# Scores of the dilated head pairs: second and third batch in one step, without projection products between them

## The chip, the cores and the metric

The kernel runs on one core of a Trainium2 chip (trn2). The metric is device time in microseconds (us): the median of three runs is 1185.5 us (1185.36 to 1185.55). One more execution was taken by the hardware profiler, and all rows below are from it. The engines are named as the profile names them: PE (TensorE, matrix products; PEld is its weight load), DVE (VectorE), ACT (ScalarE), POOL (GpSimd, nearly unused here) and SP (SyncE, which only issues transfers).

## What is computed

A decoder trunk of two layers for 512 tokens of width 1024, in float32. Layer 0 is attention and a convolutional feed-forward network, layer 1 a gated linear recurrence and another such network. The change lies in the attention of layer 0. Its queries, keys and values come from one projection of the normalised input; queries and keys are normalised per head. There are two kinds of heads:

```
oa = dilated_mixture_attention(qa, ka, va, slopes[:8])       # 8 heads of 64
ob = differential_attention(qb, kb, vb, slopes[8:], lam)     # 4 heads, two score maps each
y  = concatenate([oa, rms_norm(ob) * (1 - lam_init)]) @ w_out
```

Each dilated head mixes three windowed softmaxes. For 512 tokens the mixture is one causal softmax with an added bias for distance and for the number of windows that hold a position, and so the kernel computes it: scores q k^T, plus bias, row maximum, exponential, row sum, division, product with v.

## The kernel before

All large products are made in three parts: each operand is split into a rounded high part and a remainder (hi, lo), and PE adds hi·hi, hi·lo and lo·hi in a PSUM bank. Weights stream from HBM in units; ACT makes the high part (`wh`, line 106), DVE the remainder (`wl`, line 108).

**The attention stage as one line of steps.** The 8 dilated and 8 differential score maps are handled as 8 pairs. `ORDER = (4, 5, 6, 7, 0, 1, 2, 3)` puts four differential pairs first, then four dilated pairs, called D0, D1, D2 and D3 from here on. The backbone of PE's order is a list of *groups*: for each pair 16 groups of six projection products (`pj`, line 361), four groups to each of four weight units. The last four groups of a pair complete its four PSUM accumulators, one for each block of 128 tokens. While one pair is projected, the attention steps of the pair before are put between the groups, at places that a table gives, counted in groups from the pair's end:

```
BATCHES = ((0, 1), (2,), (3,))
PLACES = dict(qk=9, sc=(12, 14, 16), tr=(18.5, 20.7, 23.5, 25.2), step=1, out=27.3, norm=29)
```

D3 has a table of its own, `LAST`, with tighter places; beside it run the first products of the attention's output projection (`mm<-oh`, lines 127 to 129), three to a step. PE runs the list in just this order (`keep_in_program_order`). ACT and DVE get their order from a scheduler that follows the program, and that puts the evacuation of projections ahead (`high_priority`).

**One score batch** (`sc`, then `products`, lines 447 to 467). For a block of 128 query tokens there are three parts by two heads; the two heads lie on partitions 0 to 63 and 64 to 127 and write two banks. So a batch is six matmuls with a 64-row operand for each block. The first batch holds blocks 0 and 1 (128 and 256 keys), the second block 2 (384), the third block 3 (512). Each call of `products` takes two banks of the PSUM pool `pa`, which has four in all. The same pool serves the transposes of queries and keys (`qkt`), the transposes of the probabilities (`pt`), the products with v (`O`) and the row means of the differential pairs (`obms`). A tile keeps its bank until its last reader is done.

**Softmax of a row block** (`softmax_row`, line 475): DVE reads the score bank, adds the bias and keeps the negated row maximum (one instruction, followed by a short read of the accumulator, `mx`); ACT takes the exponential and the row sum; DVE the reciprocal; ACT scales. Once DVE has read a block's scores, the bank is free.

**What else ACT and DVE do there.** The evacuation of each finished projection accumulator is an ACT copy (`qkraw`, line 380), an ACT scaling (`v`, line 394) and a DVE remainder (`v`, line 395). After two accumulators, ACT squares them (`sq`, line 411) and DVE sums the squares (`ms`, line 412). Of the pair before, the second head's product with v (`O`) is read by ACT (`t`, line 561) and then by DVE (`o`, line 562).

Of the kernel before, what the change touches and what calls it, by code (L numbers as in the profile page):

```python
# [30 lines left out]


BATCHES = ((0, 1), (2,), (3,))
PLACES = dict(qk=9, sc=(12, 14, 16), tr=(18.5, 20.7, 23.5, 25.2), step=1, out=27.3, norm=29)
LAST = dict(qk=7.5, sc=(9.8, 10.5, 11.2), tr=(12.7, 13.4, 14.2, 15), step=0.35, out=16.2, norm=18)

# [28 lines left out]
def trunk(  # L65
# [30 lines left out]
    def nm(s):  # L96
        uid[0] += 1
        return f"{s}{uid[0]}"

    def bank(s):  # L100
        return pa.tile([P, S], F32, tag="pa", name=nm(s))
# [124 lines left out]
    with ExitStack() as actx:  # L226
# [73 lines left out]
        tiles = [{} for _ in ORDER]  # L300

        def pe(ins):

            return tc.keep_in_program_order(ins)
# [136 lines left out]
        def where(n):  # L441
            return LAST if n == NT - 1 else PLACES

        def head_bias(h):
            bt = ap2.tile([P, S], F32, tag="bias", name=nm("bias"))
            if h < 8:
                V.scalar_tensor_tensor(bt, dist_a, -SLOPES[h], lnc, ALU.mult, ALU.add)
            else:
                V.tensor_scalar(bt, dist_b, -SLOPES[h], None, ALU.mult)
            return bt  # L450

        def products(qk, blocks):


            (qh, ql), (kh, kl) = qk
            banks = (bank("S"), bank("S"))
            res, at = {}, 0
            for i in blocks:
                n = (i + 1) * P
                qs = slice(i * P, (i + 1) * P)  # L460
                for j, (q, k) in enumerate(((qh, kh), (ql, kh), (qh, kl))):
                    for s in range(2):
                        hs = slice(s * HD, (s + 1) * HD)
                        pe(T.matmul(banks[s][:, at : at + n], q[hs, qs], k[hs, :n], start=j == 0, stop=j == 2))  # L464
                for s in range(2):
                    res[s, i] = banks[s][:, at : at + n]
                at += n
            return res

        def softmax_row(ps, i, bt):  # L470

            n = (i + 1) * P
            e = smp.tile([P, n], F32, tag=f"sm{i}", name=nm("sm"))
            mx = tiny.tile([P, 1], F32, tag="mx", name=nm("mx"))
            V.tensor_tensor_reduce(out=e[:, :n], in0=ps, in1=bt[:, S - n :], scale=-1.0, scalar=3e38,
                                   op0=ALU.add, op1=ALU.min, accum_out=mx)
            sm = tiny.tile([P, 1], F32, tag="sum", name=nm("sum"))
            A.activation(e[:, :n], e[:, :n], AF.Exp, scale=-1.0, bias=mx, accum_out=sm)  # L478
            V.reciprocal(sm, sm)
            return e, sm  # L480

        def transposed(e, i, pth, ptl):
            ps = bank("pt")
            for b in range(i + 1):
                pe(T.transpose(ps[:, b * P : (b + 1) * P], e[:, b * P : (b + 1) * P], ident))  # L485
            src = ps[:, : (i + 1) * P].rearrange("p (b q) -> p b q", q=P)
            sl = slice(i, i + 3 * i + 1, 3)
            A.copy(pth[:, sl], src)
            return V.tensor_tensor(ptl[:, sl], src, pth[:, sl].bitcast(F32), ALU.subtract)

        def pv(out, v, pth, ptl, s=None):

            def product(b, v_cols, p, rows, start, stop):
                q = slice(b * P, S)
                rhs = p[:, 4 * b : 3 * b + NB].rearrange("p b q -> p (b q)")
                pe(T.matmul(out[rows, q], v[:, b, v_cols], rhs, start=start, stop=stop))  # L496


            every, hi, lo = slice(0, P), slice(0, P), slice(P, 2 * P)
            if s is None:  # L500
                for b in range(NB):
                    product(b, hi, pth, every, b == 0, False)
                    product(b, lo, pth, every, False, False)
                for b in range(NB):
                    product(b, hi, ptl, every, False, b == NB - 1)
            else:
                both, high = slice(s * P, (s + 1) * P), slice(s * P, s * P + HD)
                for b in range(NB - 1):
                    product(b, both, pth, every, b == 0, False)
                for b in range(NB):  # L510
                    product(b, high, ptl, slice(0, HD), False, False)
                product(NB - 1, both, pth, every, False, True)

        def pt_tiles():
            return (ap2.tile([P, 13, P], F32R, tag="pth", name=nm("pth")),
                    ap2.tile([P, 13, P], F32R, tag="ptl", name=nm("ptl")))

        def o_tiles(p):
            hi = actp.tile([P, S], F32R, tag=f"ah{p}", name=nm("oh"))
            lo = actp.tile([P, S], F32R, tag=f"al{p}", name=nm("ol"))  # L520
            oT[p] = (hi, lo)
            return hi, lo

        def attn_a(n):

            p = ORDER[n]
            st = {}

            def sc(blocks):
                if blocks[0] == 0:  # L530

                    with ExitStack() as order:
                        if n - 1 in rows_done:
                            order.enter_context(tc.issue_after(rows_done[n - 1].ins))
                        st["b"] = [head_bias(2 * p + s) for s in range(2)]
                rows = products(tiles[n]["qk"], blocks)
                for i in blocks:
                    for s in range(2):
                        e, r = softmax_row(rows[s, i], i, st["b"][s])
                        if n == NT - 1 and i == NB - 1:  # L540

                            V.tensor_scalar(e, e, r, None, ALU.mult)
                        else:
                            A.activation(e, e, AF.Copy, scale=r)  # L544
                        st["e", s, i] = e

            def tr(s, i):
                if i == 0:
                    st["pt", s] = pt_tiles()
                last = transposed(st["e", s, i], i, *st["pt", s])  # L550
                if i == 1:
                    rows_done[n] = last

            def out(s):
                ps = bank("O")
                pv(ps, tiles[n]["v"], *st["pt", s], s)
                if s == 0:
                    st["o"] = smp.tile([P, S], F32, tag="o", name=nm("o"), bufs=1)
                    st["t"] = smp.tile([P, S], F32, tag="t", name=nm("t"), bufs=1)
                lo_half, own = ((ps[HD:], slice(0, HD)), (ps[:HD], slice(HD, P)))[s]  # L560
                A.copy(st["t"][own], lo_half)
                V.tensor_tensor(st["o"][own], ps[own], st["t"][own], ALU.add)
                if s == 1:
                    hi, lo = o_tiles(p)
                    A.copy(hi, st["o"])
                    V.tensor_tensor(lo, st["o"], hi.bitcast(F32), ALU.subtract)

            at = where(n)
            steps = [(g, partial(sc, b)) for g, b in zip(at["sc"], BATCHES)]
            steps += [(g + s * at["step"], partial(tr, s, i)) for i, g in enumerate(at["tr"]) for s in range(2)]  # L570
            return steps + [(at["out"] + s * at["step"], partial(out, s)) for s in range(2)]

        def attn_b(n):
# [52 lines left out]
            at = where(n)  # L626
            steps = [(g, partial(sc, b)) for g, b in zip(at["sc"], BATCHES)]
            steps += [(g, partial(tr, i)) for i, g in enumerate(at["tr"])]
# [26 lines left out]
        at = {}  # L655
# [17 lines left out]
        for n in range(NT):  # L673
            end = 16 * n + 15
# [354 lines left out]
```

## Time and profile before

| | |
|---|---|
| Median of three runs | 1185.5 us |
| The profiled execution | 1184.98 us |
| Its span (first to last instruction) | 1183.2 us |
| PE busy | 1177.0 us, 99% of the span |
| DVE, ACT busy | 812.6 us (69%), 584.7 us (49%) |
| Attention stage | about the first 230 us |
| Granted TensorE clock, mean | 0.999 of full speed |

The timeline view gives, for each instruction, its start from the span's beginning, its duration, engine, line, operation, what it writes and reads, its shape, and in brackets the idle time of the engine before it and what ended that. Durations of matmuls overlap (the engine is pipelined), so the pace of PE is read from the differences of starts. An instruction that appears with `x2` stands for two equal ones in a row: the two heads.

### The profile page before, as it was taken

To read this page: it belongs to the slowest core of one execution; us is meant where nothing else is said; L and a number is where in the kernel's file an instruction comes from. 1 tells how busy PE (TensorE), PEld (TensorE's weight loads), DVE (VectorE), ACT (ScalarE), POOL (GpSimd) and SP (SyncE) were. 2 spreads that over 40 slices of the span, in tenths; PEclk is the share of its full clock that TensorE was granted. 3 is DMA by queue.
4 is the path that set the end of the run, shared out by engine and by line. 5 is a ranking of instruction groups with operands and counts; after the bars stand their busy time and mean duration, and the time that the engine had idled before them with its cause. 6 is when DMAs were issued, how large, how long until landed. Compare 5 with 4: busy or idle time off the path is not lost.

```text
span 1183.2 us, 14649 instructions
## 1 busy us (share of the span) xinstructions
PE 1177.0 (99%) x5568; PEld 989.4 (84%) x5568; DVE 812.6 (69%) x1330; ACT 584.7 (49%) x951; POOL 1.2 (0%) x10
## 2 busy tenths in 40 slices
PE   9999999999999999999999999999999999999998
PEld 9988988788888888888888888888888888888887
DVE  7888888777777753677346989768777763677431
ACT  7577787754444432444225698445444431444120
POOL 0000000000000000000000000000000000000000
PEclk9999999999999999999999999999999999999999
DMA  7211122153323232322323203332323323232321
GB/s 271 81 59 62 55 85 72 53 179 99 97 93 104 89 107 89 104 93 95 102 90 132 94 27 121 110 105 89 105 91 96 100 91 105 89 106 90 99 80 54
DMA packets 34198, 114.31 MB, mean 97 GB/s; under 512 B 3920, under 2 KB 4944, under 8 KB 34128
## 3 DMA queue, kind: packets, MB, share of 16 engines
q1 hardware_dynamic: 33840, 113.24, 29.6%
q8 instruction: 44, 0.72, 0.2%
q14 instruction: 26, 0.21, 0.1%
q10 hardware_dynamic: 288, 0.14, 0.0%
HBM read 111.27 MB, written 2.10 MB: 96 GB/s over the span
## 4 chain that ended last, share of the span: by engine, by line
PE 96%; ACT 2%; issue 1%; DVE 1%; DMA 0%; POOL 0%; DVEq 0%; POOLq 0%; ACTq 0%
PE mm L127 27%; PE mm L129 27%; PE mm L128 27%; PE pj L361 10%; PE O L496 1%; PE S L464 1%; PE pt L485 1%; ACT sm L478 1%; PE qkt L430 1%; ACT sm L544 1%; DMA xr<-in_xT_dram 0%; ACT v L394 0%; ACT sq L411 0%; ACT qkraw L380 0%; PE pr L127 0%
## 5 line engine op out<-in xcount | busy, mean ns | idle before, releaser
L106 ACT CAST wh<-raw 128x1024 fp32r<-128x1024 f32 (+1 forms) x204 | 208.2, 1023 | 284.2 <-PE mm L128 258.7
L129 PE MATMUL mm<-xh,wl 128*128 128x512 f32 x896 | 348.6, 389 | 0.0
L128 PE MATMUL mm<-xl,wh 128*128 128x512 f32 x896 | 348.6, 389 | 0.0
L127 PE MATMUL mm<-xh,wh 128*128 128x512 f32 x896 | 348.6, 389 | 0.0
L108 DVE TENSOR_TENSOR wl<-raw,wh 128x1024 fp32r<-128x1024 f32 (+1 forms) x204 | 241.9, 1187 | 38.7 <-ACT wh L106 35.1
L129 PEld LDWEIGHTS mm<-xh,wl 128*128 128x128 f32 x896 | 168.2, 188 | 35.2
L127 PEld LDWEIGHTS mm<-xh,wh 128*128 128x128 f32 x896 | 168.2, 188 | 35.1
L128 PEld LDWEIGHTS mm<-xl,wh 128*128 128x128 f32 x896 | 168.2, 188 | 34.7
L743 DVE SCALAR_TENSOR_TENSOR cv<-us,pt,cv 128x511 f32<-128x511 f32 (+2 forms) x216 | 160.5, 747 | 4.1 <-ACT cv L741 0.5
L127 PE MATMUL mm<-fh,wh 128*128 128x512 f32 x384 | 149.4, 389 | 0.0
L128 PE MATMUL mm<-fl,wh 128*128 128x512 f32 x384 | 149.4, 389 | 0.0
L129 PE MATMUL mm<-fh,wl 128*128 128x512 f32 x384 | 149.4, 389 | 0.0
L739 DVE TENSOR_TENSOR us<-mm,rs 128x512 f32<-128x512 f32 x104 | 71.6, 688 | 93.9 <-PE mm L129 93.6
L775 DVE TENSOR_TENSOR h<-mm,h 128x512 f32<-128x512 f32 (+1 forms) x49 | 33.2, 680 | 141.5 <-PE mm L129 141.5
L764 ACT CAST fh<-cv 128x512 fp32r<-128x512 f32 x48 | 29.8, 621 | 126.4 <-DVE cv L761 126.4
L361 PE MATMUL pj<-wh,xh 128*128 128x384 f32 x256 | 89.4, 357 | 0.1
L129 PEld LDWEIGHTS mm<-fh,wl 128*128 128x128 f32 x384 | 72.1, 188 | 15.1
L128 PEld LDWEIGHTS mm<-fl,wh 128*128 128x128 f32 x384 | 72.1, 188 | 15.0
L741 ACT ACTIVATE cv<-us,pt 128x512 f32<-128x512 f32 x104 | 84.2, 812 | 0.8 <-DVE us L739 0.6
L361 PE MATMUL pj<-wl,xh 128*128 128x384 f32 x256 | 84.3, 337 | 0.2 <-DVE wl L332 0.2
L127 PEld LDWEIGHTS mm<-fh,wh 128*128 128x128 f32 x384 | 72.1, 188 | 14.8
L361 PE MATMUL pj<-wh,xl 128*128 128x384 f32 x256 | 84.1, 336 | 0.0
(198 smaller groups left out, 1231.2 us busy)
## 6 DMA issues: line engine op xcount, KB each, us to landing
raw<-in_w_up_dram SPq DMA_DIRECT2D x96, 512.0 KB, 3.5
raw<-in_w_dn_dram SPq DMA_DIRECT2D x48, 512.0 KB, 3.5
raw<-in_w_att_dram SPq DMA_DIRECT2D x30, 384.0 KB, 3.2
raw<-in_w_ri_dram SPq DMA_DIRECT2D x16, 512.0 KB, 3.5
raw<-in_w_ao_dram SPq DMA_DIRECT2D x8, 512.0 KB, 3.9
raw<-in_w_ro_dram SPq DMA_DIRECT2D x8, 512.0 KB, 3.5
raw<-in_xT_dram SPq DMA_DIRECT2D x4, 512.0 KB, 4.1
out_dram<-h SPq DMA_DIRECT2D x7, 256.0 KB, 2.0
```

The source lines that it names most:

```text
L106: A.copy(hi, src)
L108: V.tensor_tensor(lo, src, hi.bitcast(F32), ALU.subtract)
L127: order(T.matmul(out, wh, xh, start=first, stop=False))
L128: order(T.matmul(out, wh, xl, start=False, stop=False))
L129: return order(T.matmul(out, wl, xh, start=False, stop=last))
L361: pe(T.matmul(t["banks"][bb][:, :CW], x[:, bb * P : (bb + 1) * P], w[:, j * CW : (j + 1) * CW], start=k == 0 and i == 0, stop=k == KC - 1 ...
L430: pe(T.transpose(ps[:, b * P : (b + 1) * P], raw[:, b, i], ident))
L739: V.tensor_tensor(u, ps, state["rs"], ALU.mult)
L741: A.activation(c, u, AF.Identity, scale=col(wcol + (taps - 1) * stride), bias=col(bcol))
L743: V.scalar_tensor_tensor(c[:, d:], u[:, : S - d], col(wcol + (taps - 1 - d) * stride), c[:, d:], ALU.mult, ALU.add)
L764: A.copy(hi, cg)
L775: V.tensor_tensor(h[m][:, t], ps[:, t], h[m][:, t], ALU.add)
```

## The change

The second and the third batch of the dilated pairs become one step. It stands half way between the two old places (group 15 in place of 14 and 16; in `LAST` 10.85 in place of 10.5 and 11.2). The step calls `products` twice, so it asks for four banks, and only then are the softmax rows of both blocks issued. The differential pairs keep their three batches.

```diff
+DILATED_BATCHES = ((BATCHES[0],), BATCHES[1:])
...
-            def sc(blocks):
-                if blocks[0] == 0:
+            def sc(batches):
+                if batches[0] == BATCHES[0]:
...
-                rows = products(tiles[n]["qk"], blocks)
-                for i in blocks:
+                rows = {}
+                for blocks in batches:
+                    rows.update(products(tiles[n]["qk"], blocks))
+                for i in sum(batches, ()):
                     for s in range(2):
                         e, r = softmax_row(rows[s, i], i, st["b"][s])
...
-            steps = [(g, partial(sc, b)) for g, b in zip(at["sc"], BATCHES)]
+            first, mid, end = at["sc"]
+            steps = [(g, partial(sc, b)) for g, b in zip((first, (mid + end) / 2), DILATED_BATCHES)]
```

The order on PE at D2, before: the second batch (scores `S_2621` and `S_2622`, one for each head), then twelve projection products, then the third batch (`S_2665`, `S_2666`).

```order
L464 MATMUL S_2621<-ql_2487,qh_2476 128x384
L464 MATMUL S_2622<-ql_2487,qh_2476 128x384
L361 MATMUL pj_2363<-wh_2414,xh_211 128x384
...
L464 MATMUL S_2665<-qh_2485,qh_2476 128x512
L464 MATMUL S_2666<-qh_2485,qh_2476 128x512
```

The same place on PE in the changed kernel: `S_2634` and `S_2635` are the second batch, `S_2642` and `S_2643` the third. The note at a row's end says that it waits for a count of DVE's instructions.

```order
L466 MATMUL S_2634<-qh_2485,qh_2476 128x384 [waits DVE_49]
L466 MATMUL S_2635<-qh_2485,qh_2476 128x384 [waits DVE_49]
...
L466 MATMUL S_2634<-ql_2487,qh_2476 128x384
L466 MATMUL S_2635<-ql_2487,qh_2476 128x384
L466 MATMUL S_2642<-qh_2485,qh_2476 128x512 [waits DVE_49]
L466 MATMUL S_2643<-qh_2485,qh_2476 128x512 [waits DVE_49]
```

One group of projection products that stood behind the second batch now stands ahead of it, and one that stood ahead of the third batch now stands behind it; nothing is between the batches.

The order on DVE at D2, before: `S_2621` is read behind the remainders `v` of the next pair's accumulators `pj_2361` and `pj_2362`; `o` reads the bank of the product `O_2580` of D1.

```order
L395 SCALAR_TENSOR_TENSOR v_2608<-pj_2361,rstd,v_2608 128x2x64
L479 RECIPROCAL sum_2576<-sum_2576 128x1
L395 SCALAR_TENSOR_TENSOR v_2608<-pj_2362,rstd,v_2608 128x2x64
L475 ISA sm_2629,mx_2630<-S_2621,bias_2534 128x384
L475 ISA mx_2630 128x1
L412 TENSOR_REDUCE ms_2643<-sq_2644 128x8
L562 TENSOR_TENSOR o_2524<-O_2580,t_2525 64x512
```

The same place on DVE in the changed kernel:

```order
L397 SCALAR_TENSOR_TENSOR v_2608<-pj_2362,rstd,v_2608 128x2x64
L414 TENSOR_REDUCE ms_2621<-sq_2622 128x8
L397 SCALAR_TENSOR_TENSOR v_2608<-pj_2363,rstd,v_2608 128x2x64
L477 ISA sm_2650,mx_2651<-S_2634,bias_2534 128x384
L477 ISA mx_2651 128x1
L566 TENSOR_TENSOR o_2524<-O_2580,t_2525 64x512
L477 ISA sm_2657,mx_2658<-S_2635,bias_2536 128x384
L477 ISA mx_2658 128x1
```

The sum of squares `ms` and the remainder `v` of a third accumulator (`pj_2363`) have moved ahead of the first read of the second batch's scores; the read of `O_2580` has stayed behind it. On ACT, the copy and the scaling of `pj_2363` have likewise moved up, to right behind the squares `sq`.

## Rows read from the trace of the kernel before

**Rows 1.** The page: busy time, granted clock in 40 slices, chain that ended last

```profile
PE 1177.0 (99%) x5568; PEld 989.4 (84%) x5568; DVE 812.6 (69%) x1330; ACT 584.7 (49%) x951; POOL 1.2 (0%) x10
...
PEclk9999999999999999999999999999999999999999
...
PE 96%; ACT 2%; issue 1%; DVE 1%; DMA 0%; POOL 0%; DVEq 0%; POOLq 0%; ACTq 0%
```

**Rows 2.** Timeline of PE at D2: start us, us, engine, line, operation

```profile
190.14 0.34 PE L361 MATMUL pj<-wl,xh 128*128 128x384 f32 x1
190.41 0.44 PE L464 MATMUL S<-qh,qh 64*128 64x384 f32 x2
190.69 0.34 PE L464 MATMUL S<-qh,ql 64*128 64x384 f32 x2
190.86 0.34 PE L464 MATMUL S<-ql,qh 64*128 64x384 f32 x2
191.13 0.45 PE L361 MATMUL pj<-wh,xh 128*128 128x384 f32 x1
191.42 0.34 PE L361 MATMUL pj<-wh,xl 128*128 128x384 f32 x1
...
193.42 0.51 PE L464 MATMUL S<-qh,qh 64*128 64x512 f32 x2
```

**Rows 3.** Timeline of DVE at D2

```profile
192.56 0.35 DVE L395 SCALAR_TENSOR_TENSOR v<-pj,rstd,v 128x128 fp32r<-128x128 f32 x1 [0.37 <-ACT v L394]
192.82 0.55 DVE L475 CUSTOM_DVE_ANT_0 sm<-S,bias 128x384 f32<-128x384 f32 x1
193.30 0.08 DVE L475 DVE_READ_ACCUMULATOR2_ANT mx<- 128x1 f32 x1
```

**Rows 4.** Timeline of ACT at D2

```profile
192.40 0.65 ACT L411 ACTIVATE sq<-qkraw 128x512 f32<-128x512 f32 x1
192.92 0.52 ACT L544 ACTIVATE sm<-sm,sum 128x256 f32<-128x256 f32 x1
...
194.67 0.35 ACT L380 COPY qkraw<-pj 128x256 f32<-128x256 f32 x1
194.92 0.37 ACT L394 ACTIVATE v<-pj,rstd 128x128 fp32r<-128x128 f32 x1
```

**Rows 5.** Timeline of all engines at D0

```profile
138.34 0.45 PE L464 MATMUL S<-qh,qh 64*128 64x384 f32 x2
...
139.95 0.63 ACT L411 ACTIVATE sq<-qkraw 128x512 f32<-128x512 f32 x1
...
140.61 0.69 DVE L412 TENSOR_REDUCE ms<-sq 128x8 f32<-128x512 f32 x1
```

**Rows 6.** Timeline of all engines at D1

```profile
164.84 0.44 PE L464 MATMUL S<-qh,qh 64*128 64x384 f32 x2
...
166.75 0.64 ACT L411 ACTIVATE sq<-qkraw 128x512 f32<-128x512 f32 x1
...
167.42 0.69 DVE L412 TENSOR_REDUCE ms<-sq 128x8 f32<-128x512 f32 x1 [0.17 <-ACT sq L411]
```

**Rows 7.** Timeline of PE and DVE at D3

```profile
208.91 0.39 PE L129 MATMUL mm<-oh,wl 128*128 128x512 f32 x1
...
209.14 0.60 PE L485 MATMUL pt<-ident,sm 128*128 128x128 f32 x4
...
209.67 0.44 PE L464 MATMUL S<-qh,qh 64*128 64x384 f32 x2
...
210.13 0.34 PE L464 MATMUL S<-ql,qh 64*128 64x384 f32 x2
...
210.52 0.56 DVE L475 CUSTOM_DVE_ANT_0 sm<-S,bias 128x384 f32<-128x384 f32 x1
```

**Rows 8.** Timeline of PE, the two places where it waits for a bank

```profile
149.00 0.41 PE L485 MATMUL pt<-ident,sm 128*128 128x128 f32 x2 [0.76 <-ACT pth L488]
...
202.47 0.33 PE L485 MATMUL pt<-ident,sm 128*128 128x128 f32 x1 [0.29 <-DVE ptl L489]
```

## The prediction, made before the changed kernel ran

> **What bounds the kernel now.** I read the page first [rows 1]. PE is busy for 99% of the span, the chain that ended last runs through PE for 96% of it, and the clock is at full speed in every slice. A change is therefore worth what it takes from or adds to PE's own sequence, and nothing else. The timeline of PE shows what a score batch costs there [rows 2], and the timelines of DVE and ACT [rows 3 to 7] show when a score bank is read and so comes free. PE itself has only two waits for a bank worth naming between D0's scores and the end of the stage [rows 8], 0.76 and 0.29 us. So the stage is tuned to the edge, and both sides of the change are some tenths of a us or a few us.
>
> **What is removed: one switch of PE from 128-row to 64-row operands and back, per dilated pair.** At D2 [rows 2] the batch is entered in 0.27 us (190.14 to 190.41). Two parts inside it are 0.17 apart (190.69 to 190.86). It is left in 0.27 (to 191.13), and the first product behind it takes 0.29 to the next (191.42). The pace of the products follows from the same rows: from 191.13 to 193.42 there are two groups, with one such slow start (0.11 too much) and one such entry (0.09 too much) among them, so a group is (2.29 - 0.20) / 2 = 1.045 us and a product 0.174. If the third batch follows directly, the second costs no entry of its own (0.27 - 0.17 = 0.09), no exit (0.27 - 0.17 = 0.09) and no slow start behind it (0.11): 0.29 us for each pair, four pairs, 1.2 us. The trace has no step from a 384-column to a 512-column score block; by the nearest rows it lies between 0.17 (inside the batch) and 0.27 (leaving it). At the upper end the four pairs save 0.8 us; I take 1.2, since the operands keep their shape of 64 rows. For D3 I use the same figure.
>
> **What is added: a wait for a bank in the middle of each merged step.** The step asks for four banks of a pool of four, but one bank is always held by something else. At D1 and D2 it is the second head's product O of the pair before: PE makes it right behind the first score batch, and in the order on DVE in the changed kernel its read `o` stands behind the first read of the merged step. At D0 it is the row means of the last differential pair, whose reader on DVE stands even further back; at D3 it is the transposes `pt` ahead of the step. So three banks serve four score tiles, and the fourth tile (third batch, second head) has to take the bank of the first one (second batch, first head) as soon as DVE has read it. Before, this reuse was there too, but two groups of products later: at D2 DVE finished that read at 193.38 [rows 3] and the third batch went at 193.42 [rows 2], so the cover was just used up. Now nothing covers it. Behind the waiting matmul stand all of PE's later instructions, in program order.
>
> How long does PE wait? First when it is ready. The second batch stands one group later than before, 1.045 us, and the fourth tile's first matmul is due 0.45 (first to last part, 190.41 to 190.86) + 0.17 = 0.62 behind the batch's start. From the starts 138.34, 164.84 and 190.41 [rows 5, 6, 2] it is due at 140.01, 166.51 and 192.08.
>
> Then when the read is done. In the new order on DVE the sum of squares and the remainder of the third accumulator stand ahead of it, at D0 to D2 alike. Up to the squares on ACT nothing moves. They end at 139.95 + 0.63 = 140.58 (D0), 166.75 + 0.64 = 167.39 (D1) and 192.40 + 0.65 = 193.05 (D2) [rows 5, 6, 4]. From there:
> - the sum of squares starts 0.03 later (140.61 and 167.42) and lasts 0.69; the next DVE instruction starts some 0.08 before the one ahead ends (192.56 + 0.35 = 192.91 against 192.82) [rows 3]: 0.03 + 0.61;
> - the remainder `v` takes 0.26 to the next start [rows 3]. Its input is there: ACT goes on 0.52 after the squares' start, its copy takes 0.25 and its scaling 0.37 [rows 4], in all 1.14 after the squares' start or 0.5 after their end;
> - the read of 384 columns takes 0.55, and the short read behind it ends 0.01 later; PE follows 0.04 to 0.06 later, as at 193.38 to 193.42.
>
> That is 0.03 + 0.61 + 0.26 + 0.55 + 0.06 = 1.51 behind the squares: 142.09, 168.90, 194.56. PE loses 2.1, 2.4 and 2.5 us.
>
> At D3 there are no evacuations ahead of the read, and the three output products pass in front of the batch; at 0.23 each (208.91 to 209.14) it starts at 209.67 + 0.7 = 210.37. There the read ended 210.52 + 0.56 + 0.01 = 211.09, or 0.96 behind the last part's start at 210.13 [rows 7]. PE needs its tile 0.17 behind that start, so it loses 0.96 + 0.05 - 0.17 = 0.8 us. This is the least such a wait can cost. The four waits make 7.8 us. From below they are bounded by 0.8 each, 3.3; from above I allow 1 us more for what comes late.
>
> **What comes after.** In a wait, ACT and DVE lose less than PE, since part of their work goes on, but the rows of both blocks now fall into one stretch. The two old waits [rows 8] may go, because PE arrives there some 2 us later, or stay, because DVE is late too: between -1.05 and 0, and if DVE stays behind at the products O and the next transposes, a new wait of up to 1 us. I take -0.5, half of what the two rows hold. Everything else moves without a price: the second batch one group later and the third one group earlier still leave three groups before the first transposes; the weights are split two units ahead; the transfers on SP are the same and in the same order. Behind the attention stage PE alone sets the pace, so the loss is not given back.
>
> **Sum.** 7.8 - 1.2 - 0.5 = +6.1 us. The profiled execution took 1184.98 us (span 1183.2), so 1191.1 on its scale; it lies 0.5 under the median of the runs, on whose scale I forecast 1191.6.
>
> **Rivals.**
> 1. *The read is prompt at all four pairs.* If ACT and DVE reach the first row of the merged step without the queue ahead of it, each wait costs the least, 0.8 as at D3: 3.3 - 1.2 - 0.5 = +1.6, 1187.1, which is not told apart from no change. The point from which it decides: the read would have to be done about 1 us behind the second batch's last part. For it speaks only D3; against it the order on DVE and the squares' end at D0 to D2, which alone lies 0.6 to 1.0 behind the time at which PE is due.
> 2. *No wait, because the four tiles find four free banks.* Then only the gains stand: -1.2 - 1.05 = -2.2, 1183.3, at the edge of faster. Against it: the read of O behind the first row in the order on DVE, and the third batch at 193.42 right behind the read at 193.38.
> 3. *The clock falls.* PE has no idle time near 2 us in the trace behind its first product, the longest is 0.76 us, and the granted clock is at its upper level (2.4 GHz) throughout [rows 1, 8]; three idle stretches of 2.1 to 2.5 us are new. If the clock went to 1.2 GHz for about as long as each of them, half of 2.1 + 2.4 + 2.5 would be lost on top, +3.5: 1195. The Trainium skill, "TensorE: Matmul & The Clock Gate", section on the HAM clock gate, says that idle time sends the clock to half speed and that it has to be earned back. The trace neither shows nor excludes that for 2 us.
> 4. *The delay spreads.* DVE stays behind and PE waits again at the products O or the transposes of each pair: +0.5 to +1 at D0, D1 and D2, 1194.
>
> **How the numbers follow.** Forecast 0.78; rival 1: 0.12; rival 2: 0.02; rival 3: 0.04; rival 4: 0.04. What a measurement of this kernel can tell from no change is about 0.2%, 2.4 us: 1183.1 to 1187.9. The forecast and rivals 3 and 4 are slower, and of rival 1 about a sixth: 0.88. Same is the rest of rival 1 and half of rival 2, rounded to 0.10, and faster 0.02. The range leaves out rivals 1 and 2 and the far side of rival 3: its low end, 1187.9 or +2.4, has waits of 4.65 in all (1.2 on the mean) with both old waits gone (4.65 - 1.2 - 1.05); its high end, 1194 or +8.5, has waits of 8.8, the lower saving of 0.8 and a new wait of 0.5.
>
> **What would show it.** Right: in the changed kernel PE has, at each dilated pair, a gap of 2.1, 2.4, 2.5 and 0.8 us between the first and the second matmul of the 512-column block, ended by DVE's read of the 384-column scores; the second batch runs into the third at 0.17 to 0.27. The gaps at 149 and 202 us are smaller or gone, and from 230 us on all is shifted by the whole loss at the same pace. Wrong: no such gap, gaps under 1 us at D0 to D2 (rival 1), products at half pace behind the gaps (rival 3), or longer waits at transposes and O (rival 4).

## The result, and the profile after

The changed kernel takes 1192.4 us, the median of four executions (1190.17 to 1194.35); the kernel before takes 1185.5 us beside it (four, 1185.36 to 1185.55). The ratio is 1.0059, with a 95% interval of 1.0047 to 1.0071: slower by about 0.6%. The forecast was 1191.6, with a range of 1187.9 to 1194.0. The spread is new: the four executions lie at 1190.17, 1191.68, 1193.14 and 1194.35 us, 1.2 to 1.5 us apart (the kernel before lies within 0.2 us here, and within 1.2 us over the 21 executions of the first set below), and their mean granted clocks are 1.000, 0.999, 0.997 and 0.996 in the same order. A mean of 0.999 alone says little, since the kernel before has it too: there the clock falls only behind the last matmul. The profiled execution is the one of 1191.68 us.

The page of the changed kernel, the rows that answer to [rows 1]:

```profile
span 1189.9 us, 14649 instructions
...
PE 1178.9 (99%) x5568; PEld 993.3 (83%) x5568; DVE 814.1 (68%) x1330; ACT 586.4 (49%) x951; POOL 1.5 (0%) x10
...
PEclk9999999999999999999999999999999999999999
...
PE 97%; ACT 1%; DVE 0%; issue 0%; DVEq 0%
```

The span is 6.7 us longer, PE is busy for only 1.9 us more, and the page alone shows nothing else: the shares are the same, and 40 slices of 30 us are too coarse for anything of 3 us. The place has to be read from the views of the stage.

PE's waits from 20 to 240 us, of the changed kernel (engine, line, what for: us in total, times, longest):

```profile
PE S L466 <- DVE mx L477: 6.2, 4, 2.1
```

This is the only row. The two old waits of [rows 8], both at `pt`, are gone; in their place stand four waits of a score matmul for DVE's read of the scores. The timeline of PE at D2 shows one of them (answers to [rows 2]; all lines are two higher than before):

```profile
196.00 0.34 PE L363 MATMUL pj<-wl,xh 128*128 128x384 f32 x1
196.27 0.44 PE L466 MATMUL S<-qh,qh 64*128 64x384 f32 x2
196.54 0.34 PE L466 MATMUL S<-qh,ql 64*128 64x384 f32 x2
196.72 0.34 PE L466 MATMUL S<-ql,qh 64*128 64x384 f32 x2
196.90 0.39 PE L466 MATMUL S<-qh,qh 64*128 64x512 f32 x1
199.37 0.50 PE L466 MATMUL S<-qh,qh 64*128 64x512 f32 x1 [2.09 <-DVE mx L477]
```

The last two rows were one row with `x2` before. The first head's 512-column matmul goes 0.18 us behind the 384-column batch, so the step really has lost its switch; the second head's goes 2.47 us later. The bracket says 2.09, since the matmul ahead counts as busy for 0.39 us; what PE loses is the difference of the starts (in the kernel before the two heads' matmuls start together, one row with `x2`). DVE in the same stretch (answers to [rows 3]):

```profile
197.90 0.69 DVE L414 TENSOR_REDUCE ms<-sq 128x8 f32<-128x512 f32 x1 [0.17 <-ACT sq L413]
198.50 0.34 DVE L397 SCALAR_TENSOR_TENSOR v<-pj,rstd,v 128x128 fp32r<-128x128 f32 x1
198.76 0.55 DVE L477 CUSTOM_DVE_ANT_0 sm<-S,bias 128x384 f32<-128x384 f32 x1
199.23 0.09 DVE L477 DVE_READ_ACCUMULATOR2_ANT mx<- 128x1 f32 x1
```

The queue is the one that the order showed: sum of squares, remainder `v`, and only then the read that PE waits for. Scores that were complete before 197.1 are read from 198.76 on. The read ends at 199.32 and PE goes 0.05 later.

Now the clock. Table of stretches of the changed kernel around D0's wait (window; us; busy us and instructions of PE, PEld, DVE, ACT, POOL; granted clock; share and GB/s of DMA):

```profile
140.00:142.40 2.40, 0.77 (x7) 0.39 (x5) 1.87 (x7) 2.40 (x9) 0.00 (x0) 1.00 0.00 0
142.40:144.00 1.60, 1.57 (x7) 1.18 (x8) 1.46 (x6) 1.60 (x4) 0.00 (x0) 0.79 0.00 0
144.00:146.00 2.00, 2.00 (x7) 2.00 (x7) 1.35 (x4) 1.39 (x6) 0.00 (x0) 0.50 0.03 8
146.00:148.00 2.00, 2.00 (x11) 2.00 (x11) 1.69 (x4) 2.00 (x6) 0.00 (x0) 0.81 0.02 4
148.00:150.00 2.00, 2.00 (x14) 1.93 (x13) 2.00 (x8) 2.00 (x7) 0.00 (x0) 1.00 0.00 0
```

Behind a wait in which PE had 0.77 us of work in 2.4, the granted clock falls to 0.50 (1.2 GHz) and comes back to 1.00 (2.4 GHz) before 148. PE counts as busy in all of it: a slow clock is not seen as idle time, but in the pace of the starts (0.32 us for each product from 143.79 to 146.67 below, 0.17 to 0.18 at 1.00). PE's timeline behind D0's wait (two rows of scores and eight of products left out):

```profile
142.43 0.50 PE L466 MATMUL S<-qh,qh 64*128 64x512 f32 x1 [1.66 <-DVE mx L477]
...
143.30 0.69 PE L363 MATMUL pj<-wh,xh 128*128 128x384 f32 x1
143.79 0.52 PE L363 MATMUL pj<-wh,xl 128*128 128x384 f32 x1
...
146.67 0.37 PE L363 MATMUL pj<-wh,xl 128*128 128x384 f32 x1
```

and behind D1's wait in the same execution, which is longer:

```profile
171.63 0.50 PE L466 MATMUL S<-qh,qh 64*128 64x512 f32 x1 [2.01 <-DVE mx L477]
...
172.53 0.44 PE L363 MATMUL pj<-wh,xh 128*128 128x384 f32 x1
172.80 0.34 PE L363 MATMUL pj<-wh,xl 128*128 128x384 f32 x1
172.98 0.35 PE L363 MATMUL pj<-wl,xh 128*128 128x384 f32 x1
```

From 143.30 to 146.67 ten products take 3.37 us. At the pace behind D1 they take 0.27 + 9 x 0.174 = 1.84. So this fall costs 1.5 us, which is also about the step between the executions: their times fit none to three falls, but only this one was seen in a trace. D1's and D2's longer waits are followed by full pace here.

**The balance.** The four differences of starts at the 512-column block are 2.04, 2.40, 2.47 and 0.82 us, 7.73 in all. The switch saves 4 x 0.29 = 1.17 by the prediction's figure. The two old waits give back 0.92 + 0.45 = 1.37 (counted below), and the fall of the clock takes 1.5. 7.73 - 1.17 - 1.37 + 1.5 = 6.7 us, which is the difference of the two spans (1189.9 - 1183.2). Without the fall it is 5.2, on the 1184.98 of before 1190.2; the execution whose mean clock is 1.000 took 1190.17.

It closes this well partly by luck. The starts of the same matmul in both traces show 0.35 us of the difference already ahead of the merged steps (the first product behind D0's first score batch starts at 135.29 before and at 135.64 after), and 0.24 us come back at D3's transposes (four of them, from 217.81 to the next product at 218.40 before, from 224.74 to 225.09 after); neither is in the sum. Counted in this way D1 costs 2.09 us and D2 2.17, so a merged step with a wait saves 0.3 us, as put in. From 230 us to the end nothing more changes: the matmul at 229.48 before is the one at 236.19 after, the last one stands at 1179.16 and at 1185.87, 6.71 us later both times.

### The profile page after: what moved, and what is told of

It is laid out like the page before. It is cut to its first block, busy times and chain, and to the rows that moved or that the text cites. A ratio compares the mean times of both kernels' runs of the same rounds, so it can differ in the third digit from the quotient of the medians.

```text
span 1189.9 us, 14649 instructions
## 1 busy us (share of the span) xinstructions
PE 1178.9 (99%) x5568; PEld 993.3 (83%) x5568; DVE 814.1 (68%) x1330; ACT 586.4 (49%) x951; POOL 1.5 (0%) x10
## 4 chain that ended last, share of the span: by engine, by line
PE 97%; ACT 1%; DVE 0%; issue 0%; DVEq 0%
PE mm L129 27%; PE mm L130 27%; PE mm L131 27%; PE pj L363 11%; PE S L466 1%; PE O L498 1%; PE pt L487 1%; PE qkt L432 1%; ACT sm L480 0%; PE warm L651 0%; ACT sm L548 0%; DVE sm L477 0%; PE pr L129 0%; PE pr L131 0%; PE pi L130 0%
```

## The experiments

Eight kernels ran in two sets. Medians are over 5 to 11 executions; the kernel before ran beside them, 1185.06 us in the first set (21 executions, 1184.65 to 1185.86) and 1185.25 in the second (29, 1184.43 to 1185.86).

**1. Free banks for D1 and D2.** Only these two have the merged step, and the second head's O of D0 and of D1 is made ahead of the next pair's first score batch, so that its bank is free when the four are asked for.

```diff
+MERGED = (5, 6)
...
+            second = 28.0 if n + 1 in MERGED else at["out"] + at["step"]
```

> D1 and D2 have the merged step, D0 and D3 keep three batches. At D1 and D2 the second head's product O of the pair before stands ahead of the first score batch in place of behind it, so its bank is read long before the merged step and the four score tiles get four banks that are free. Theory (the loss is the wait for the reused bank): no gap inside the merged steps, step from second to third batch 0.17 us, 0.29 us saved at each of the two pairs, so 1184.9 us, +-0.4, and the granted clock 1.000 in every execution. Rival (the loss comes from the softmax rows of two blocks falling into one stretch of DVE and ACT, whatever the banks): PE waits later at transposes or products O, 1188 us or more.

Measured: 1185.07 us (1184.66 to 1185.44), ratio 0.9999 (0.9991 to 1.0008). PE at D2 in this kernel, the merged step without a gap:

```profile
191.99 0.35 PE L467 MATMUL S<-ql,qh 64*128 64x384 f32 x2
192.17 0.41 PE L467 MATMUL S<-qh,qh 64*128 64x512 f32 x2
192.41 0.40 PE L467 MATMUL S<-qh,ql 64*128 64x512 f32 x2
192.64 0.40 PE L467 MATMUL S<-ql,qh 64*128 64x512 f32 x2
192.97 0.44 PE L364 MATMUL pj<-wh,xh 128*128 128x384 f32 x1
```

The second batch runs into the third in 0.18 us, both heads together. The bank held by O was thus the cause of the waits at D1 and D2: with it free they are gone, and run 3 has them with O where it was. What the merge then saves doesn't arrive as a whole; see run 2.

**2. The control for it: O ahead, three batches everywhere.**

```diff
-                steps = [(g, partial(sc, b)) for g, b in zip((first, (mid + end) / 2), DILATED_BATCHES)]
+                steps = [(g, partial(sc, (b,))) for g, b in zip(at["sc"], BATCHES)]
```

> The kernel before (three batches at every dilated pair) with the product O of D0 and of D1, second head, ahead of the next pair's first score batch: the other half of the run above. Both theories: 1185.5 us, +-0.5; what it differs from the kernel before is taken off the run above.

Measured: 1185.47 us (1184.83 to 1185.98), ratio 1.0004 (0.9995 to 1.0013). The two merges of run 1 are worth 0.4 us in the medians against this control, where 2 x 0.29 = 0.58 was expected; the ranges overlap. Moving O by itself can't be told from no change.

The traces of both runs show what the medians can't. The same two products around D1's second and third batch, in run 1 and then here:

```profile
163.15 0.34 PE L364 MATMUL pj<-wh,xl 128*128 128x384 f32 x1
...
169.63 0.33 PE L364 MATMUL pj<-wl,xh 128*128 128x384 f32 x1
```

```profile
163.13 0.34 PE L364 MATMUL pj<-wh,xl 128*128 128x384 f32 x1
...
170.01 0.33 PE L364 MATMUL pj<-wl,xh 128*128 128x384 f32 x1
```

PE needs 6.48 us with the merge and 6.88 without it; at D2 it needs 4.98 (190.06 to 195.04) and 5.37 (189.82 to 195.19). So a merge with free banks saves 0.4 us, more than the 0.29 worked out. Later waits take part of it back: at 182.15 run 1 waits at transposes (0.50 by the bracket) that go at 181.94 without a wait here, while at 203.41 this control waits longer than run 1 does at 202.22 (0.62 and 0.36). This fits the rival of run 1 in part: with the rows of two blocks in one stretch, a later step waits.

**3. The other control: D1 and D2 merged, O where the change has it.**

```diff
+MERGED = (5, 6)
...
+            if n in MERGED:
+                steps = [(g, partial(sc, b)) for g, b in zip((first, (mid + end) / 2), DILATED_BATCHES)]
+            else:
+                steps = [(g, partial(sc, (b,))) for g, b in zip(at["sc"], BATCHES)]
```

> D1 and D2 merged as in the changed kernel, D0 and D3 with three batches, O where it was. Theory: two gaps of 2.4 and 2.5 us, 0.6 us saved, the old wait of 0.45 us at 202 us gone, the one at 149 us (0.92 us of pace) left: 1185.5 + 4.9 - 0.6 - 0.45 = 1189.3 us in an execution whose clock stays up, and about 1.5 us more for each time that it falls, so some executions at 1190.8 or 1192.3. Rival (rows in one stretch): the same gaps need not be there, and the run with O ahead is no faster than this one.

Measured: 1192.16 us, ratio 1.0057 (1.0044 to 1.0070), with executions at 1189.98, 1190.36, 1192.16, 1193.00 and 1193.57. So two merged steps alone bring a loss and a spread as large as those of the changed kernel, though by another mix: fewer waits, and a lower clock in each of the five executions (means of 0.996 to 0.998). The profiled execution, the slowest, in PE's waits and in the table of stretches:

```profile
PE S L467 <- DVE mx L478: 4.1, 2, 2.1
PE pt L488 <- ACT pth L491: 0.8, 1, 0.8
```

```profile
171.00:174.00 3.00, 3.00 (x11) 3.00 (x11) 2.69 (x9) 2.89 (x8) 0.00 (x0) 0.50 0.00 0
...
198.40:201.00 2.60, 2.50 (x8) 1.75 (x9) 2.47 (x9) 2.54 (x7) 0.00 (x0) 0.50 0.00 0
201.00:204.00 3.00, 3.00 (x10) 2.61 (x9) 1.54 (x6) 1.69 (x6) 0.00 (x0) 0.50 0.01 3
```

The starts lie 2.39 us apart at D1 and 2.47 at D2, as in the changed kernel, and here both waits bring the lower clock, D2's for twice as long. The old wait at `pth` stands as before, since D0 has no merged step here; the one at `ptl` (0.45 us) is gone. The waits less the saving and less this one make 2.39 + 2.47 - 0.58 - 0.45 = 3.8, on the 1185.06 of before 1188.9; the other 4.7 us of this execution are left for the clock and for the ordinary differences between executions.

**4. Work in the wait.** The changed kernel, with seven matmuls of 512 columns between the second and the third batch at D0, D1 and D2. They write into the bank of the third batch's first head, which its first matmul overwrites; the output doesn't use them.

```diff
+            for _ in range(fill):
+                pe(T.matmul(banks[0], ones_r, xs[0][0], start=True, stop=True))
```

> The changed kernel with seven 512-column products more at each of D0, D1 and D2, between the second and the third batch; they write the third batch's first tile, which its own first matmul then overwrites. They add nothing to the result and fill some 1.6 to 1.8 us of the wait. Theory (gaps in PE of 2 us let the clock fall in some executions, and each fall costs about 1.5 us): gaps of 0.3 to 0.9 us, clock 1.000 and 1190.2 us +-0.4 in every execution, with a spread under 0.5 us, although PE has more to do. Rival (the spread of 1190.2 to 1194.4 us has another cause): the times stay spread over 3 us or more, and 21 more products cost time on top.

Measured: 1190.1 us (1189.47 to 1190.45), ratio 1.0041 (1.0029 to 1.0054), mean clock 1.000 in all five. 21 matmuls more, and 2.3 us less than the changed kernel's median (1.9 less when each is taken against the kernel before that ran beside it, 5.0 and 6.9); the executions lie 1 us apart, not 4. The spread under 0.5 us that was expected was too narrow: the kernel before spreads 1.2 us itself. PE at D0 in this kernel:

```profile
139.66 1.91 PE L461 MATMUL S<-xh,ones_r 128*128 128x512 f32 x7
...
142.51 0.44 PE L364 MATMUL pj<-wh,xh 128*128 128x384 f32 x1
142.80 0.34 PE L364 MATMUL pj<-wh,xl 128*128 128x384 f32 x1
```

The filling shortens nothing: from the first score matmul of the merged step to the first product behind it D0 takes 3.58 us here (138.93 to 142.51) and 3.55 in the changed kernel (139.75 to 143.30). What differs is the pace behind it. The time is that of the balance without a fall, 1190.2. So the spread and about 2 us of the median loss come from the clock, and the clock falls because PE waits, not because of the merge.

**5. The queue ahead of the read.** The changed kernel, with the first softmax row of the merged step issued ahead of the evacuations.

```diff
-                        e, r = softmax_row(rows[s, i], i, st["b"][s])
+                        with tc.high_priority() if i == 2 and s == 0 else ExitStack():
+                            e, r = softmax_row(rows[s, i], i, st["b"][s])
```

> The changed kernel, with the first softmax row of the merged step (block 2, first head) issued ahead of the evacuations: on DVE its read now stands ahead of the remainder v of the third accumulator at D0 and D1, still behind the sum of squares; at D2 the order stays. Theory (the queue on DVE ahead of the read sets the length of PE's wait): the gaps at D0 and D1 are shorter by the 0.26 us that the remainder holds DVE, 1.78 and 2.14 in place of 2.04 and 2.40; D2 and D3 stay at 2.48 and 0.82. The time is 0.5 us less at an equal number of clock falls: 1189.6 without a fall, 1191.1 with one. Rival (the wait is set by the scores' own latency, or by ACT): all four gaps as before, 1190.2 without a fall. If the evacuation that is passed comes late in turn, new waits appear at the qkt or pt behind, and nothing is gained.

Measured: 1191.1 us (1189.09 to 1194.83), ratio 1.0050 (1.0037 to 1.0064). DVE at D0 in the changed kernel, then in this one:

```profile
141.56 0.34 DVE L397 SCALAR_TENSOR_TENSOR v<-pj,rstd,v 128x128 fp32r<-128x128 f32 x1
141.81 0.55 DVE L477 CUSTOM_DVE_ANT_0 sm<-S,bias 128x384 f32<-128x384 f32 x1
142.29 0.09 DVE L477 DVE_READ_ACCUMULATOR2_ANT mx<- 128x1 f32 x1
```

```profile
141.05 0.69 DVE L414 TENSOR_REDUCE ms<-sq 128x8 f32<-128x512 f32 x1 [0.17 <-ACT sq L413]
141.65 0.55 DVE L477 CUSTOM_DVE_ANT_0 sm<-S,bias 128x384 f32<-128x384 f32 x1
142.12 0.08 DVE L477 DVE_READ_ACCUMULATOR2_ANT mx<- 128x1 f32 x1
142.12 0.35 DVE L397 SCALAR_TENSOR_TENSOR v<-pj,rstd,v 128x128 fp32r<-128x128 f32 x1
```

The read now comes right behind the sum of squares, and the starts on PE lie 1.81 us apart at D0 and 2.14 at D1 (expected 1.78 and 2.14), at D2 and D3 as in the changed kernel. So what stands on DVE ahead of the read is part of the wait: taking the remainder away shortens it by 0.23 and 0.26 us. The sum of squares was not moved. The medians can't show 0.5 us in this spread; the gaps do. In the profiled execution (1191.28 us) the clock falls again behind D0's wait, though it is only 1.8 us long, and there alone, as in the profiled one of the changed kernel (1191.68 us): 0.4 us between the two.

**6. D3 alone.** Only D3 has the merged step (`MERGED = (7,)` in the diff of run 3).

> Only D3 has the merged step; D0, D1 and D2 have three batches as before the change. Theory (a merged step costs its wait, less 0.29 us of the switch it saves; a fall of the clock needs one of the gaps over 2 us): gap of 0.82 at D3, +0.5 us in all, 1185.6 against 1185.1, not told apart from no change; clock 1.0 in every execution, times within 0.6 us; the old waits at 149 and 202 us stay as they were. Rival (each merge costs the same, or any gap brings the clock down): a quarter of the loss of the changed kernel, +1.7, 1186.8, and a spread of 1.5 us between executions.

Measured: 1185.67 us (1185.09 to 1185.93), ratio 1.0002 (0.9994 to 1.0011). PE at D3 in this kernel:

```profile
211.07 0.39 PE L467 MATMUL S<-qh,qh 64*128 64x512 f32 x1
211.88 0.49 PE L467 MATMUL S<-qh,qh 64*128 64x512 f32 x1 [0.42 <-DVE mx L478]
```

The wait of 0.8 us is there, and +0.4 us on the median agrees with 0.82 - 0.29, though it can't be told from none. All eleven executions lie within 0.84 us, with no steps of 1.5: in none of them is there a sign that this wait brought the clock down.

**7 and 8. Can the merge pay?** Run 1 still has three waits at transposes, at 148.83, 182.15 and 202.22; the first and the last stand in the kernel before too. In PE's waits of run 1 they make two rows:

```profile
PE pt L488 <- DVE ptl L492: 0.9, 2, 0.5
PE pt L488 <- ACT pth L491: 0.8, 1, 0.8
```

So its transposes were moved later, and, for comparison, those of the kernel before (there without the entry for `(5, 3, 1)`, and with O where it was).

```diff
+LATER = {(4, 1, 1): 1, (5, 3, 1): 1, (6, 2, 0): 0.7}
-LAST = dict(qk=7.5, ...
+LAST = dict(qk=8.2, ...
...
-            steps += [(g + s * at["step"], partial(tr, s, i)) ...
+            steps += [(g + s * at["step"] + LATER.get((n, i, s), 0), partial(tr, s, i)) ...
```

> D1 and D2 merged, with the second head's O of D0 and D1 ahead of the next pair's scores so that four banks are free (as in the run that came out equal to before), D0 and D3 with three batches; and the three steps at which PE waited there are moved later: the second head's transposes of block 1 at D0 (wait at 148.8 us) and of block 3 at D1 (182.2) by one group, and at D2 the first head's transposes of block 2 with D3's qkt (202.2) by one group of output products. Theory (the merges' saving of 0.29 us each was eaten by waits at transposes, which are a matter of place): the three waits are gone, 0.92 + 0.66 + 0.58 us = 2.2 less than that run's 1185.1: 1182.9. Rival (the rows of both blocks in one stretch make ACT and DVE late as a whole, so a wait only moves to the next step): new waits of the same size behind, about 1185.

> The kernel before, three batches everywhere, with the two steps moved at which its PE waits: the second head's transposes of block 1 at D0 by one group, and at D2 the first head's transposes of block 2 with D3's qkt by one group of output products. It is the control for the run with merged D1 and D2 and later transposes. Theory: both waits gone, 0.92 + 0.45 us less than before: 1183.7; the other run is then 0.6 to 0.8 faster than this one if a merge with free banks saves 0.29 us. Rival: merges save nothing once the waits are moved, and the two runs are equal; or the waits move on to the next steps, about 1185.

Measured: with merged D1 and D2 1184.36 us (1183.55 to 1184.88), ratio 0.9992 (0.9984 to 1.0001); with three batches 1184.80 (1184.32 to 1184.96), ratio 0.9995 (0.9987 to 1.0004). PE in the merged version, then in the other:

```profile
183.63 0.80 PE L500 MATMUL O<-ptl,v 128*64 128x512 f32 x4 [0.39 <-DVE ptl L493]
...
205.37 0.66 PE L489 MATMUL pt<-ident,sm 128*128 128x128 f32 x4 [0.42 <-DVE ptl L493]
```

```profile
205.40 0.66 PE L486 MATMUL pt<-ident,sm 128*128 128x128 f32 x4 [0.36 <-DVE ptl L490]
```

Neither theory holds as a whole. The wait at 149 is gone from both; the one at 182 has moved to the next O at 183.6, and the one at 202 to the next transposes at 205.4. The merged version is 0.44 us ahead of this comparison, which also differs in the place of O; in runs 1 and 2 it was 0.40. Of the 0.8 us that two merges with free banks save by the traces of runs 1 and 2, about half arrives in the time. The merged version has the lowest median of all kernels here, 0.9 us under the kernel before, but its interval touches 1, so that it is faster is likely and not shown.

## Why the prediction was right, step by step

**What bounds the kernel: right.** PE's own sequence set the time: what was lost or saved on it appears in the span, and the sum of four terms closes to 0.1 us (helped by the 0.35 and 0.24 us above, which nearly cancel). Nothing was given back behind the stage: 6.71 us at 230 us and at the end.

**The switch that is saved: right.** Second to third batch takes 0.18 us (forecast 0.17), and the step needs one entry and one exit. At the merged steps with a wait 0.3 us is what the starts of the same matmuls leave, as forecast. With free banks it is 0.4 (runs 1 and 2): the sum had counted the slow first product behind a batch, but not the slow first pair at its head (0.28 us from 190.41 to 190.69 in [rows 2], where the next takes 0.17). The doubt about the step from 384 to 512 columns, up to 0.27 us, did not come true.

**The four waits: right in cause and size.** Forecast 2.1, 2.4, 2.5 and 0.8 us, measured 2.04, 2.40, 2.47 and 0.82. Runs 1 and 3 show that the bank held by O makes those of D1 and D2, run 5 that one instruction queued on DVE makes 0.23 and 0.26 us of those at D0 and D1. For D0 and D3 the tenant of the bank (`obms`, `pt`) was not moved in a run. The trace of the changed kernel agrees with it: DVE's last read of `obms` starts at 144.59 (line 623) and that of `pt` at 218.70 (line 491), behind the ends of the waits at 142.43 and 218.22.

**The old waits: the term that was mis-sized.** The prediction bounded them by -1.05 and took -0.5; both went, and they were worth -1.37. Two things failed. Taking half of the bound had no row behind it, and it cost 0.55. The other 0.32 lies in how [rows 8] was read: the bracket counts only idle time, from the modelled end of the matmul ahead. From start to start PE lost 1.10 - 0.17 = 0.92 us at 149.00 and 0.68 - 0.23 = 0.45 at 202.47, the normal step subtracted. For the new waits this was done rightly: they were priced from when PE was due.

**The clock: a rival with 0.04 that came true in part.** The forecast counted on the upper level throughout. Three of four executions have a lower mean clock, and the profiled one falls to 0.50 right behind a wait, as rival 3 describes it: products at half pace behind the gaps. Its price was not the 3.5 us put there, for two reasons. Not every wait is followed by a fall; and a fall lasts longer than the wait that brings it, about 3.4 us behind the 2.04 of D0, so it costs about 1.5 us and not half of the wait. The sum without the clock was 0.9 too high. On the scale of the medians the balance without a fall gives 1185.5 + 5.2 = 1190.7, so the median has 1.7 us of clock on top, and the forecast's distance of 0.8 us is the difference of these two. That it came so near is luck: the errors have opposite signs. The rule of the Trainium skill quoted there ("TensorE: Matmul & The Clock Gate", section on the HAM clock gate) fits what these traces show, from 1.00 to 0.50 behind a wait and back; the rival built on it deserved more weight than it was given.

**The other rivals.** The prompt read and the four free banks did not occur. The delay does not spread either: PE has no wait in the stage but the four. (With the banks free, in run 1, a later wait of 0.5 us does appear.)

## What to carry to other kernels

Before two steps that take buffers from one pool are put together, count who holds the buffers at that moment in the order of the readers: four banks asked for from a pool of four are three if an older tenant is read later, and the price is the reader with all that is queued ahead of it: 0.8 us at D3, where nothing was, and 2.0 to 2.5 at D0 to D2. A wait on TensorE costs the difference of starts less the normal step, and where it grows to about 2 us, look at the granted clock behind it in more than one execution. A wait that can't be removed can be cheaper when it is filled with work that nobody needs (run 4).

## What the hardware showed that was not expected

- Waits of 1.8 to 2.5 us (start to start) brought the granted clock from 1.00 to 0.50 in some executions and at some places, not in others: in one execution behind 2.04 us and not behind 2.40 and 2.47. The low stretches seen in the attention stage lasted about 3.4 us (three of them, in the changed kernel and in runs 3 and 5) and about 6.8 us (one, in run 3). Which wait it happens behind is not settled by these runs.
- Waits of 0.8 to 1.1 us from start to start (149.00 in the kernel before, 205.37 in run 7) were followed by no such stretch in the profiled executions, and the executions of each of these kernels lie within 1.5 us of each other.
- Seven idle-filling matmuls in each of three waits made the kernel about 2 us faster than with the waits empty (1190.1 against 1192.4 in the medians), with a mean clock of 1.000 in all five executions.
